# When operands from and for DRAM are loaded in a split-precision encoder block: three places in the order of DMA loads

## The chip, the cores and the metric

The kernel runs on one core of a Trainium2 chip. The time is the device time in microseconds (us) from start to end of one execution; of several executions the median is given. The engines are named as the profile names them: PE is the matrix engine (PEld its weight loads), DVE the vector engine, ACT the scalar engine, POOL the engine that runs GpSimd's work, SP the one that here only issues DMA transfers. Each engine works its own list of instructions strictly in order and waits on semaphores where an operand isn't there yet. DMA transfers are issued by SP and POOL, also in the order of their lists.

## The reference

One encoder block on x of 1024 rows by 1024 columns, float32. Cut to its core:

```python
x = layer_norm(DN_ALPHA * x + 0.5 * swiglu(x, ffn1_w_gate, ffn1_w_up, ffn1_w_down), ln1_g, ln1_b)
z = x @ w_in                                       # q, k, v, forget gates, and the RG-LRU's columns
fox = forgetting_attention(q, k, v, fg)            # 8 heads of 64, causal, logits + cum[t] - cum[s]
lru = gelu(z[..., LG_OFF:LG_OFF + LRU_W]) * rg_lru(causal_depthwise_conv(z[..., LX_OFF:LX_OFF + LRU_W]))
mix = concatenate([fox, lru]) @ w_out
x = layer_norm(DN_ALPHA * x + mix, ln2_g, ln2_b)
x = layer_norm(DN_ALPHA * x + 0.5 * swiglu(x, ffn2_w_gate, ffn2_w_up, ffn2_w_down), ln3_g, ln3_b)
# swiglu: (silu(x @ w_gate) * (x @ w_up)) @ w_down, with a hidden width of 4096
```

## The kernel before

**Arithmetic.** Every float32 operand is split into a high part (a cast to fp32r on ACT, about 0.62 us for 128x512) and a low part (the operand less its high part, on DVE, about 0.69 us). A product of two operands is three matmuls, high by high, high by low and low by high (L163, L164, L165 of `mm3`). The big products of the two FFNs are done on quarters of the matrices with seven products instead of eight (the steps `one` to `seven`, `s1` to `s4` and `t1` to `t4` are the sums that this scheme needs). All of this loads PE, and the splits load ACT and DVE.

**FFN 1, gate and up** (`gate_up`) runs over 16 pairs of weight blocks. For a pair, `weights` loads gate's and up's raw columns (L364, 1 MB each, into one of two `raw` buffers) and makes the operands of the products from them. Pair 0 has a function of its own, `first_pair`, whose order on PE, DVE and ACT is the order of the code (`manual_schedule`): the helper `put` makes a high part at L385 and notes the low part, which `do` makes later at L391. L443 copies a transposed block of x to SBUF, L449 adds two such blocks. Everywhere else a list scheduler of the framework orders the instructions of each engine, by the program's order and by what it expects of the instructions' times. `issue_after(x)` tells it to put what is made inside behind x.

**Work for later, spread over the pairs.** `prepare` is a generator (`steps`). Between its yields it makes, in small pieces, the operands of FFN 2's pair 0 and writes them to DRAM (`pre_d`), then the split halves of one part of W_out and writes these to DRAM as well (`wo_d`). A step loads a small tile (`aux`, L272), subtracts (L290, L296, L302, L307), splits it in `halves` and stores it through POOL's DMA queue (L285, L317). `gate_up` takes a step after `two` and after `five` of gate and of up, in each pair from pair 1 on.

**Attention** (`attention`) is a loop over 64 units (h, i): head h, block i of 128 query rows. The scores of a unit are made three units ahead of its values (`AHEAD`). `probs` makes the scores on PE (L1158, L1159), masks a part of `cum` on POOL (L1162), adds and takes the minimum on DVE (L1164), and takes the exponential on ACT (L1165). `to_pT` transposes the probabilities (PE L1179) and splits them (ACT L1183, DVE L1184). `values` multiplies them with v (PE L1200), and adds up in `o` (ACT L1203, DVE L1204). When a pair of heads is done, its output is scaled (L1188, L1209, L1210) and split into a `mix` (ACT L1212, and L1213 on POOL or DVE), which is stored to `mix_d` by POOL's queue (L1216). The heads' inputs q, k, v and `cum` are loaded on SP ahead of the head (L1139 to L1144).

Within the loop there is other work to fill PE: up to unit 35, tiles of the product of the RG-LRU's half with W_out; near the end, `out_tile`, the product of the stored mixes with W_out's other half. For it `ready_out_w` (L1119) loads the split parts of W_out from `wo_d`, two tiles of 512 KB for each of four parts, in the eight `ws` buffers that the fill tiles had before. Units 40, 50 and 52 (`MIXES`) load the three stored mixes (L1269), and unit 52 also loads the scale and shift of norm 2 (`load_gb`, L102 for the scale, L105 for the shift, tiles named `gb`); POOL then multiplies the scale by -1 (L192). The last loads of `gb` are remembered as `self.fetched`.

**FFN 2, gate and up** begins after the attention with `ready_pair`, which fetches the operands of pair 0 from `pre_d` (L556): "11", "21" and "t1" into `ws` tiles, "t4" and "t2" into the two `raw` buffers.

Of the kernel before, what the change touches and what calls it, by code (L numbers as in the profile page):

```python
# [10 lines left out]
F32R = mybir.dt.float32r  # L11
# [6 lines left out]
P = 128  # L18
# [41 lines left out]
class Block:  # L60
# [273 lines left out]
    def gate_up(self, wg, wu, h_d, rows, bank, tp, wsp, raws=None, later=None, aside=None, ready=None, steps=None):  # L334
# [4 lines left out]
        nc, v = self.nc, self.nc.vector  # L339
# [4 lines left out]
        def two_blocks():  # L344
            return block(F32R), block(F32R)
# [15 lines left out]
        def weights(pair, view, w):  # L361

            r = self.raw([P, KT, 2 * P])
            nc.sync.dma_start(r, view[:, :, pair * 2 * P:(pair + 1) * 2 * P])  # L364
            b11, b12, b21, b22 = quarters(r)
            w["11"] = parts(b11)
            w["21"] = parts(b21)
            t1 = less(b12, b11)
            t2 = less(b22, t1)
            w["t2"] = parts(t2)  # L370
            w["t1"] = parts(t1)
            w["t3"] = parts(less(b22, b12))
            w["22"] = parts(b22)
            w["t4"] = parts(less(b21, t2))
# [171 lines left out]
        def ready_pair(g, u):  # L546

            both = g, u
            r1, r2 = rows[0:4], rows[4:NT]

            def place(name, j):
                return tuple(x[:, :, j * P:(j + 1) * P] for x in A[name])

            def fetch(n, m, to):
                for l in range(2):
                    nc.sync.dma_start(f32(to[l]).rearrange("p (h k) f -> p h k f", h=2),  # L556
                                      ready[both.index(m), OPERANDS.index(n)].rearrange("h p (l k) f -> l p h k f", l=2)[l])
                m.w[n] = to

            for n in ("11", "21", "t1"):  # L560
                for m in both:
                    fetch(n, m, two_blocks())
            for n in ("t4", "t2"):
                r = self.rawp.tile([P, 4, 4, P], F32R, tag="raw", name=self.nm("raw"))
                for i, m in enumerate(both):
                    fetch(n, m, (r[:, 2 * i], r[:, 2 * i + 1]))
            t21 = [block() for _ in range(4)]
            g.sum, u.sum = self.sum_bank(), self.sum_bank()
            g.product("11", "11", g.sum, True)
            u.product("11", "11", u.sum, True)  # L570
            s = [block() for _ in range(4)]
            a22, two = {}, {}
            for n, j in enumerate((3, 2, 1, 0)):
                nc.scalar.copy(t21[j], self.transposed(r2[j], 0, bank))
                a22[j] = self.transposed(r2[j], 1, bank)
                v.tensor_tensor(s[j], a22[j], t21[j], ALU.add)
                parts(s[j], place("s1", j))
                if n < 2:
                    m = both[n]
                    nc.scalar.copy(m.s1, m.sum)  # L580
            two[g] = g.product("21", "12")
            parts(a22[3], place("22", 3))
            two[u] = u.product("21", "12")
            v.tensor_tensor(g.c[0], two[g], g.s1, ALU.add)
            for j in (2, 1, 0):
                parts(a22[j], place("22", j))
            g.z = g.product("t1", "s1")
            u.z = u.product("t1", "s1")
            v.tensor_tensor(u.c[0], two[u], u.s1, ALU.add)
            for m in both:  # L590
                fetch("t3", m, two_blocks())
            nc.scalar.copy(g.s5, g.z)
            four = {g: g.product("t4", "22")}

            def s2(j):
                v.tensor_tensor(s[j], s[j], unsplit(r1[j], 0), ALU.subtract)
                parts(s[j], place("s2", j))

            def s3(j):
                v.tensor_tensor(t21[j], unsplit(r1[j], 0), t21[j], ALU.subtract)  # L600
                parts(t21[j], place("s3", j))

            for j in range(4):
                s2(j)
            four[u] = u.product("t4", "22")
            nc.scalar.copy(u.s5, u.z)
            nc.scalar.copy(g.c[2], four[g])
            s3(0)
            s3(1)
            g.product("t2", "s2", g.sum)  # L610
            nc.scalar.copy(u.c[2], four[u])
            u.product("t2", "s2", u.sum)
            s3(2)
            s3(3)
            for m in both:
                nc.scalar.copy(m.u, m.sum)
            for j in range(4):
                v.tensor_tensor(s[j], unsplit(r1[j], 1), s[j], ALU.subtract)
                parts(s[j], place("s4", j))
            for m in both:  # L620
                fetch("22", m, two_blocks())
            g.product("t3", "s3", g.sum)
            u.product("t3", "s3", u.sum)

            def add_seven(m):
                v.tensor_tensor(m.c[3], m.sum, m.s5, ALU.add)
                v.tensor_tensor(m.c[2], m.c[2], m.sum, ALU.add)

            for m in both:
                m.product("22", "s4", m.z)  # L630
                add_seven(m)
            for m in both:
                v.tensor_tensor(m.c[1], m.z, m.u, ALU.add)
# [48 lines left out]
        for pair in range(FF // P // 2):  # L682
            if pair == 0:
                g0, h0, first, fifth, g1, h1, u = (self.row() for _ in range(7))
                homes = list(zip(halves(first), halves(first), halves(fifth)))
                gate, up = Matrix((g0, g1), *homes[0]), Matrix((h0, h1), *homes[1])
            else:
                g0, g1, uu, h0, h1, u = (self.row() for _ in range(6))
                gate, up = (Matrix(r, r[1][:, 0:H], x, r[0][:, H:]) for r, x in zip(((g0, g1), (h0, h1)), halves(uu)))
            def finish(pair=pair, g=(g0, g1), h=(h0, h1), u=u):  # L690
                for x, y in zip(h, g):
                    v.tensor_tensor(x, x, y, ALU.mult)
                (a11, a21), (a12, a22) = (halves(x) for x in h)
                s5 = g[0][:, 0:H]
                v.tensor_tensor(u[:, 0:H], a11, a22, ALU.add)
                v.tensor_tensor(u[:, H:], a21, a22, ALU.add)  # L696
                v.tensor_tensor(s5, a11, a12, ALU.add)
                v.tensor_tensor(a21, a21, a11, ALU.subtract)
                v.tensor_tensor(a12, a12, a22, ALU.subtract)
                d = h_d[pair // 4][:, pair % 4].rearrange("r p t -> p r t")  # L700
                for n, t in enumerate((*h, u)):
                    nc.gpsimd.dma_start(d[:, 2 * n:2 * n + 2], t.rearrange("p (r t) -> p r t", r=2))  # L702
                return nc.gpsimd.dma_start(d[:, 6], s5)

            def end(pair=pair, finish=finish):
                store = finish()
                if aside is not None and pair == 2:
                    with self.tc.issue_after(store.ins):
                        aside()

            if pair == 0:
                if ready is not None:
                    ready_pair(gate, up)
                else:
                    with self.tc.manual_schedule(engines=ENGINES):
                        first_pair(gate, up)
                silu((g0, g1))
                end()
                continue
            for m, view in zip((gate, up), self.gu_views(wg, wu)):  # L720
                weights(pair, view, m.w)
            for m in (gate, up):
                m.one()
                if pending:
                    pending()
                for step in ("two", "six", "five", "seven", "three"):
                    getattr(m, step)()
                    if steps and step in ("two", "five"):
                        next(steps, None)

                def pending(m=m, gate=gate, g=(g0, g1), end=end, last=pair == FF // P // 2 - 1):
                    m.four()
                    if m is gate:
                        silu(g)
                    elif not last:
                        end()
# [385 lines left out]
    def attention(self, w_out, mixp, ln, normed):  # L1122

        nc, v = self.nc, self.nc.vector
# [5 lines left out]
        with self.pool("att_p", 3) as pp, self.pool("att_t", 1) as tp, self.pool("att_pt", 6) as ptp, self.pool("att_qk", 2, side="right") as qkp:  # L1130
# [110 lines left out]
            for n in range(len(units) + AHEAD + 1):  # L1241
                if n < len(units):
                    h, i = units[n]
# [10 lines left out]
                for m in due(n - 1):  # L1254
                    h, i = units[m]
# [4 lines left out]
                if fill and (n < 2 or n % 8 in (2, 3, 4)):  # L1260
                    i, d = fill.pop(0)
                    with self.tc.issue_after(scores.ins) if n < 3 else nullcontext():
                        self.down_tile(i, lru_tiles, 1.0, (d,))
                if 45 <= n < 53 and n % 2:
                    w_fox.append(next(w_steps))
                if n in MIXES:
                    mix.append(tuple(self.hp.tile([P, T], F32R, tag="h", name=self.nm("mix")) for _ in range(2)))
# [147 lines left out]
```

## Time and profile before

| | |
|---|---|
| median of 3 runs | 2323.25 us (2322.42 to 2323.91) |
| the profiled execution | 2323.19 us |
| its span, first to last instruction | 2321.5 us |
| mean granted clock of PE | 0.997 |
| DVE busy | 1635.6 us (70%) |
| ACT busy | 1019.1 us (44%) |
| POOL busy | 227.8 us (10%) |
| DMA, mean over the span | 139 GB/s |

The page of the profile lists busy times, the chain of work that ended last, and groups of instructions. Views of the trace show the instructions of an engine in a window (the timeline: start, duration, engine, line, operation, output<-input, shapes, how often in a row, and in brackets how long the engine had been idle and what ended it), the waits of an engine in sums (total, how many, the longest), busy time by stretch with the granted clock of PE (the share of full speed), and the chain of waits. L12 is line 12 of the kernel before. Rows with DMA_DIRECT2D on SP or POOL are issues of transfers; the chain shows how long such a transfer took to land. The first pair runs from about 10 to 60 us of the span, the attention from about 1170 to 1345 us.

### The profile page before, as it was taken

What the parts mean: (1) busy time and instruction counts of PE and PEld (TensorE: products, weight loads), DVE (VectorE), ACT (ScalarE), POOL (GpSimd) and SP (SyncE); (2) the same over time, 40 slices, a digit from 0 to 9 for tenths busy, and PEclk for the clock granted to TensorE, in tenths of its full rate; (3) what the DMA queues carried; (4) which work ended last, traced back from release to release, by engine and by line L of the source; (5) the groups of instructions that cost most, each with busy time, mean ns of one, the idle gap of its engine ahead of it and who ended that gap; (6) DMA issues with size and microseconds to landing.
All of it is one profiled execution on the core that took longest, in us unless ns stands there. A gap on an engine that the chain in (4) does not pass through costs nothing.

```text
span 2321.5 us, 28560 instructions
## 1 busy us (share of the span) xinstructions
PE 2298.7 (99%) x10705; PEld 1914.1 (82%) x10705; DVE 1635.6 (70%) x2521; ACT 1019.1 (44%) x1623; POOL 227.8 (10%) x388
## 2 busy tenths in 40 slices
PE   8999999999999999999999999999999999999998
PEld 7888888888888888888898788888888888888887
DVE  7867666666467788866667899565656665577886
ACT  5443434343344345453556755334333333344341
POOL 0121111100000000111133210000000000000000
PEclk9999999999999999999999999999999999999999
DMA  4444444433276433233274934232323232564542
GB/s 150 141 141 145 139 147 141 146 113 125 101 259 234 147 127 109 75 92 110 91 218 126 283 137 141 86 118 89 122 93 123 87 118 87 195 244 168 182 144 73
DMA packets 194444, 323.08 MB, mean 139 GB/s; under 512 B 10033, under 2 KB 115825, under 8 KB 194305
## 3 DMA queue, kind: packets, MB, share of 16 engines
q1 hardware_dynamic: 167712, 230.74, 30.9%
q0 software_dynamic: 26592, 90.51, 9.9%
q8 instruction: 84, 1.38, 0.3%
q14 instruction: 56, 0.45, 0.1%
HBM read 226.81 MB, written 94.40 MB: 138 GB/s over the span
## 4 chain that ended last, share of the span: by engine, by line
PE 81%; issue 10%; DVE 3%; DMA 3%; POOL 2%; ACT 1%; SPq 0%; POOLq 0%; DVEq 0%; ACTq 0%
PE x L163 7%; PE x L164 7%; PE x L165 7%; PE s L165 6%; PE s L164 6%; PE s L163 6%; PE a L165 6%; PE a L164 6%; PE a L163 6%; PE b L163 6%; PE b L164 6%; PE b L165 6%; PE a L1200 1%; PE a L1179 1%; PE a L1049 1%
## 5 line engine op out<-in xcount | busy, mean ns | idle before, releaser
L349 ACT CAST ws<-t 128x512 fp32r<-128x512 f32 x240 | 148.9, 623 | 374.2 <-PE b L164 253.0
L349 ACT CAST ws<-raw 128x512 fp32r<-128x512 f32 x180 | 111.0, 622 | 239.3 <-PE x L164 237.3
L350 DVE TENSOR_TENSOR ws<-t,ws 128x512 fp32r<-128x512 f32 x240 | 164.3, 686 | 56.4 <-ACT ws L349 50.6
L350 DVE TENSOR_TENSOR ws<-raw,ws 128x512 fp32r<-128x512 f32 x180 | 123.3, 688 | 114.4 <-ACT ws L349 110.3
L164 PE MATMUL a<-ws,ws 128*128 128x512 f32 x512 | 199.8, 390 | 0.2
L163 PE MATMUL a<-ws,ws 128*128 128x512 f32 x512 | 199.3, 390 | 0.4 <-ACT row L672 0.4
L163 PE MATMUL b<-As,ws 128*128 128x512 f32 x512 | 199.4, 389 | 0.2 <-ACT row L663 0.2
L164 PE MATMUL b<-As,ws 128*128 128x512 f32 x512 | 199.3, 389 | 0.0
L165 PE MATMUL b<-As,ws 128*128 128x512 f32 x512 | 199.2, 389 | 0.0
L165 PE MATMUL a<-ws,ws 128*128 128x512 f32 x512 | 199.2, 389 | 0.0
L163 PE MATMUL x<-As,ws 128*128 128x512 f32 x504 | 196.6, 390 | 2.1 <-ACT row L659 2.0
L164 PE MATMUL x<-As,ws 128*128 128x512 f32 x504 | 196.1, 389 | 0.0
L165 PE MATMUL x<-As,ws 128*128 128x512 f32 x504 | 196.1, 389 | 0.0
L163 PE MATMUL x<-A,ws 128*128 128x512 f32 x496 | 193.3, 390 | 0.0
L165 PE MATMUL x<-A,ws 128*128 128x512 f32 x496 | 193.0, 389 | 0.0
L164 PE MATMUL x<-A,ws 128*128 128x512 f32 x496 | 193.0, 389 | 0.0
L772 ACT CAST ws<-raw 128x1024 fp32r<-128x1024 f32 x112 | 117.4, 1050 | 157.8 <-PE a L164 87.2
L775 DVE TENSOR_TENSOR ws<-raw,ws 128x1024 fp32r<-128x1024 f32 x112 | 136.6, 1220 | 53.0 <-ACT ws L772 52.6
L702 POOL DMA_DIRECT2D h_d<-row x96 | 68.9, 719 | 968.5 <-DVE row L696 928.4
L163 PE MATMUL s<-ws,ws 128*128 128x512 f32 x384 | 149.5, 389 | 0.0
L165 PE MATMUL s<-ws,ws 128*128 128x512 f32 x384 | 149.4, 389 | 0.0
L164 PE MATMUL s<-ws,ws 128*128 128x512 f32 x384 | 149.4, 389 | 0.0
(295 smaller groups left out, 5252.7 us busy)
## 6 DMA issues: line engine op xcount, KB each, us to landing
raw<-h_d SPq DMA_DIRECT2D x56, 1024.0 KB, 5.4
h_d<-row POOLq DMA_DIRECT2D x96, 512.0 KB, 3.5
wd<-in_ffn_w_down_dram SPq DMA_DIRECT2D x32, 1024.0 KB, 7.5
raw<-in_ffn_w_gate_dram SPq DMA_DIRECT2D x30, 1024.0 KB, 5.3
raw<-in_ffn_w_up_dram SPq DMA_DIRECT2D x30, 1024.0 KB, 5.3
h_d<-row POOLq DMA_DIRECT2D x32, 256.0 KB, 2.7
raw<-in_w_in_dram SPq DMA_DIRECT2D x16, 512.0 KB, 4.9
pre_d<-ws POOLq DMA_DIRECT2D x28, 256.0 KB, 2.7
```

What stands on the lines that cost most here:

```text
L163: mm(out, ah, bh, start=first, stop=False, skip_group_check=goes_on)
L164: mm(out, ah, bl, start=False, stop=False, skip_group_check=goes_on)
L165: mm(out, al, bh, start=False, stop=last, skip_group_check=goes_on)
L349: nc.scalar.copy(hi, src)
L350: v.tensor_tensor(lo, src, f32(hi), ALU.subtract)
L702: nc.gpsimd.dma_start(d[:, 2 * n:2 * n + 2], t.rearrange("p (r t) -> p r t", r=2))
L772: cast = nc.scalar.copy(hi, src)
L775: self.mark = v.tensor_tensor(lo, src, f32(hi), ALU.subtract)
L1049: nc.tensor.matmul(pa[:, 0:width], xh, wh[:, 0:width], start=k == 0, stop=False)
L1179: nc.tensor.transpose(pa[:, (j % 4) * P:(j % 4 + 1) * P], p[:, j * P:(j + 1) * P], self.ident)
L1200: mm(pv[:, ps], vt[:, j, :], pts[h, qt][j // 4][l][:, j % 4, ps], start=j == 0 and l == 0, stop=j == last and l == 1)
```

## The change

```diff
@@ def gate_up: weights
-            nc.sync.dma_start(r, view[:, :, pair * 2 * P:(pair + 1) * 2 * P])
+            self.weight_load = nc.sync.dma_start(r, view[:, :, pair * 2 * P:(pair + 1) * 2 * P])
@@ def gate_up: ready_pair
-            for n in ("11", "21", "t1"):
-                for m in both:
-                    fetch(n, m, two_blocks())
-            for n in ("t4", "t2"):
-                r = self.rawp.tile([P, 4, 4, P], F32R, tag="raw", name=self.nm("raw"))
-                for i, m in enumerate(both):
-                    fetch(n, m, (r[:, 2 * i], r[:, 2 * i + 1]))
+            with self.tc.issue_after(self.fetched.ins):
+                for n in ("11", "21", "t1"):
+                    for m in both:
+                        fetch(n, m, two_blocks())
+                for n in ("t4", "t2"):
+                    r = self.rawp.tile([P, 4, 4, P], F32R, tag="raw", name=self.nm("raw"))
+                    for i, m in enumerate(both):
+                        fetch(n, m, (r[:, 2 * i], r[:, 2 * i + 1]))
@@ def gate_up: the loop over pairs
                     if steps and step in ("two", "five"):
-                        next(steps, None)
+                        with self.tc.issue_after(self.weight_load.ins):
+                            next(steps, None)
@@ def attention
-                if 45 <= n < 53 and n % 2:
+                if 36 <= n < 40:
                     w_fox.append(next(w_steps))
```

There are three edits. A step of `prepare` that is taken in a pair is put behind the last raw load of that pair. The fetches of `ready_pair` are put behind the last load of `gb`. And the four parts of W_out are asked for at units 36 to 39 instead of units 45, 47, 49 and 51. No instruction is added to the computation or taken from it. The scheduler, which has new bounds and a new program order, moves further instructions.

**The first pair, on SP.** Transfers at the start of the kernel, in the order in which SP issues them: x's rows, the first two `aux` tiles of `prepare`, and pair 1's raw columns (`raw_669` of gate, `raw_707` of up). Before:

```order
L1316 DMA x_27_134<-in_x_dram 128x1024
L272 DMA aux_773<-in_ffn_w_gate_dram 128x2x128
L272 DMA aux_775<-in_ffn_w_gate_dram 128x2x128
L364 DMA raw_669<-in_ffn_w_gate_dram 128x8x256
L364 DMA raw_707<-in_ffn_w_up_dram 128x8x256
L364 DMA raw_954<-in_ffn_w_gate_dram 128x8x256
```

And on SP with the change, at the same place:

```order
L1318 DMA x_27_134<-in_x_dram 128x1024
L364 DMA raw_669<-in_ffn_w_gate_dram 128x8x256
L364 DMA raw_707<-in_ffn_w_up_dram 128x8x256
L272 DMA aux_773<-in_ffn_w_gate_dram 128x2x128
L272 DMA aux_775<-in_ffn_w_gate_dram 128x2x128
L364 DMA raw_954<-in_ffn_w_gate_dram 128x8x256
```

The two `aux` loads stand behind the two raw loads of pair 1, which need the `raw` buffers that pair 0 reads. (Lines in the changed kernel are up to two higher.)

**The first pair, on DVE.** The subtractions of `prepare` (L290) and of the first pair, before:

```order
L391 TENSOR_TENSOR ws_176<-raw_135,ws_175 128x512
L391 TENSOR_TENSOR ws_178<-raw_136,ws_177 128x512
L290 TENSOR_TENSOR aux_775<-aux_775,aux_773 128x256
L391 TENSOR_TENSOR ws_180<-t_261,ws_179 128x512
L355 TENSOR_TENSOR t_289<-raw_135,t_261 128x512
```

With the change L290 stands on DVE among the sums of pair 1's operands (L355), 64 positions later:

```order
L350 TENSOR_TENSOR ws_676<-raw_669,ws_675 128x512
L355 TENSOR_TENSOR t_679<-raw_669 128x512
L290 TENSOR_TENSOR aux_775<-aux_775,aux_773 128x256
L355 TENSOR_TENSOR t_681<-raw_669,t_679 128x512
L544 TENSOR_TENSOR row_167<-b_632,row_164 128x512
```

Nothing of `prepare` is left in the first pair on DVE; the order of the first pair's own instructions is as it was.

**The end of the attention, on SP.** Loads of W_out's parts (`w`), of a stored mix (`mix`) and of head 6 (`q`, `kh`, `kl`, `cum`, `v`). Before, from the first mix on:

```order
L1269 DMA mix_11083<-mix_d 128x1024
L1269 DMA mix_11084<-mix_d 128x1024
L1119 DMA w_11254<-wo_d 128x1024
L1119 DMA w_11255<-wo_d 128x1024
L1140 DMA kh_11106<-k_d 64x1024
L1139 DMA q_11105<-q_d 64x1024
```

With the change SP's order at that place is:

```order
L1121 DMA w_10980<-wo_d 128x1024
L1121 DMA w_10981<-wo_d 128x1024
L1121 DMA w_11005<-wo_d 128x1024
L1121 DMA w_11006<-wo_d 128x1024
L1121 DMA w_11043<-wo_d 128x1024
L1121 DMA w_11044<-wo_d 128x1024
L1121 DMA w_11063<-wo_d 128x1024
L1121 DMA w_11064<-wo_d 128x1024
L1271 DMA mix_11099<-mix_d 128x1024
L1271 DMA mix_11100<-mix_d 128x1024
L1141 DMA q_11121<-q_d 64x1024
L1142 DMA kh_11122<-k_d 64x1024
```

All eight loads of W_out's parts stand ahead of the first mix and of head 6; before, the other six came after head 6's and head 7's loads.

**The end of the attention, on POOL.** Masks of head 6 and head 7 (`cum_11104` and `cum_11358` before, `cum_11120` and `cum_11366` with the change), copies of the scaling of an output (`gate_raw`), and the scaling of `gb` (L192). Before:

```order
L1162 AFFINE_SELECT cum_11104<-cum_11104 128x128
L1162 AFFINE_SELECT cum_11358<-cum_11358 128x128 x2
L1188 COPY gate_raw<-wfr 128x256
L192 TENSOR_SCALAR gb_11523<-gb_11523 128x1024
L1162 AFFINE_SELECT cum_11104<-cum_11104 128x128
```

With the change, on POOL:

```order
L1164 AFFINE_SELECT cum_11120<-cum_11120 128x128
L192 TENSOR_SCALAR gb_11523<-gb_11523 128x1024
L1164 AFFINE_SELECT cum_11366<-cum_11366 128x128 x2
L1190 COPY gate_raw<-wfr 128x256
L1164 AFFINE_SELECT cum_11120<-cum_11120 128x128
```

The scaling of `gb` stands ahead of two masks of head 7, those of its blocks 4 and 3, and ahead of the copy, where it stood behind all three.

**The other loads from pre_d.** The eight loads of "t4" and "t2" stood on SP among the loads of the first three heads, at two places of four; with the change they stand behind the loads of `gb`. On PE, DVE and ACT, head 6's first scores and what follows from them come 16 PE rows later, behind head 5's last values and transposes.

## The prediction

> **What bounds the kernel now.** I read the first part of the page, then the waits of TensorE, and then, at each place that the change touches, the timelines of the engines there.
>
> ```profile
> PE 2298.7 (99%) x10705; PEld 1914.1 (82%) x10705; DVE 1635.6 (70%) x2521; ACT 1019.1 (44%) x1623; POOL 227.8 (10%) x388
> ```
>
> TensorE (PE) is busy for 2298.7 of the span's 2321.5 us, so at most some 23 us could be saved without taking matmuls away, and the change takes none away. Every microsecond in which PE is held up anywhere is added to the end, and every idle stretch that goes is taken from it. The sum is thus a sum over idle stretches of PE. The waits of PE say which are worth looking at:
>
> ```profile
> PE b L163 <- ACT ws L443: 2.8, 1, 2.8
> PE s L1158 <- DVE m L1164: 2.4, 7, 0.9
> ```
>
> The largest is a single stretch of 2.8 us behind a copy of L443 in the first pair; the second is spread over seven places in the attention. The change reaches both.
>
> **First pair: the aux loads behind pair 1's raw loads.** On DVE, the subtraction L290 leaves the first pair (position 16 of its order) for pair 1 (position 80). Views: the timelines of DVE, ACT and PE, with the start, the duration and the work, and in brackets the idle time before it.
>
> ```profile
> 15.62 1.29 DVE L391 TENSOR_TENSOR ws<-raw,ws 128x512 fp32r<-128x512 f32 x2
> 19.57 0.43 DVE L290 TENSOR_TENSOR aux<-aux,aux 128x256 f32<-128x256 f32 x1 [2.66 <-DMA aux<-in_ffn_w_gate_dram]
> 19.91 0.68 DVE L391 TENSOR_TENSOR ws<-t,ws 128x512 fp32r<-128x512 f32 x1
> ...
> 22.32 1.28 DVE L449 TENSOR_TENSOR ws<-b,ws 128x512 f32<-128x512 f32 x2
> ```
>
> ```profile
> 19.33 0.60 ACT L443 COPY ws<-b 128x512 f32<-128x512 f32 x1
> 23.04 0.62 ACT L385 CAST As<-ws 128x512 fp32r<-128x512 f32 x1 [3.11 <-DVE ws L449]
> 23.56 0.58 ACT L443 COPY ws<-b 128x512 f32<-128x512 f32 x1
> ```
>
> ```profile
> 17.73 3.66 PE L249 MATMUL b<-ident,x 128*128 128x128 f32 x32
> 24.19 0.50 PE L163 MATMUL b<-A,ws 128*128 128x512 f32 x1 [2.80 <-ACT ws L443]
> ...
> 25.71 0.63 PE L163 MATMUL b<-A,ws 128*128 128x512 f32 x1
> ```
>
> DVE stands still for 2.66 us until an aux tile has landed. Behind it everything is late in a row: L449 at 22.32, ACT's cast at 23.04, ACT's next L443 at 23.56, and PE, whose transposes ended at 17.73 + 3.66 = 21.39, gets its bank only at 24.19. Without L290 the DVE row of 19.91 follows the pair of 15.62, less the usual 0.08 of overlap, at 16.83: DVE gains 3.08. L449 then starts at 19.24, the cast at about 19.96 (ACT is free at 19.93), L443 at 20.48, and the bank is free at about 21.1, ahead of 21.39. So PE's stretch of 2.80 goes.
>
> PE gains something besides. Right behind the stretch stand rows of 0.63 us where the others have 0.39:
>
> ```profile
> 22.20:25.60 3.40, 1.41 (x6) 1.20 (x7) 3.31 (x7) 2.56 (x5) 0.00 (x0) 1.00 0.00 0
> 25.60:29.00 3.40, 3.40 (x10) 2.67 (x9) 2.96 (x5) 2.63 (x6) 0.00 (x0) 0.50 0.00 0
> 29.00:32.40 3.40, 3.40 (x16) 2.79 (x16) 2.84 (x6) 0.00 (x0) 0.00 (x0) 1.00 0.00 0
> ```
>
> In these stretches the busy times of PE, PEld, DVE, ACT and POOL are followed by the granted clock: 1.00, then 0.50, then 1.00. At half clock PE did 10 matmuls where it does 16 otherwise, which is 6 x 0.23, or about 1.5 us. I read this as the answer to the pause, so it goes too. PE alone would gain 2.80 + 1.5 = 4.3 us.
>
> But PE isn't alone here. At the end of the first pair DVE delivers just in time (DVE's row, PE's row, and from the view of L436 on DVE what it had waited for between 28 and 32, in us and times):
>
> ```profile
> 56.97 0.68 DVE L391 TENSOR_TENSOR As<-ws,As 128x512 fp32r<-128x512 f32 x1
> ```
>
> ```profile
> 57.71 0.50 PE L164 MATMUL b<-As,ws 128*128 128x512 f32 x1
> ```
>
> ```profile
>   PE b L165: 0.9, 2
> ```
>
> DVE's last operand is done at 57.65 and PE's row that reads it starts at 57.71, with no slack. DVE comes forward by 3.08 and by what its own two waits for PE (0.9 us) shrink, since PE is earlier by more than DVE. I take about half of these: **-3.5 us**. Bounds: -2.9 (nothing of the waits, and some of L290's 0.43 us comes back as lateness in pair 1, where DVE is packed) and -4.3 (PE's whole gain).
>
> In pair 1, L290 stands between two L355. Its loads leave SP behind the two raw loads, of which this is the second:
>
> ```profile
> 50.30 0.39 SPq L364 DMA_DIRECT2D raw<-in_ffn_w_up_dram  x1
> ```
>
> ```profile
> 62.47 0.69 DVE L355 TENSOR_TENSOR t<-raw,t 128x512 f32<-128x512 f32 x1
> ```
>
> ```profile
> 11.03 8.45 DMA aux<-in_ffn_w_gate_dram
> ```
>
> Issued at about 51 in before's time, with the 8.45 us that they took in the chain of waits, they land near 59.5, ahead of 62. No wait comes back; only 2 to 3 us of slack stand against it. The other pairs keep their order.
>
> **Gate/up 2's operands behind norm 2's vectors.** Eight raw loads from pre_d move on SP from two places in the early attention to behind the loads of gb.
>
> ```profile
> 1162.95 2.03 SPq L556 DMA_DIRECT2D raw<-pre_d  x4
> 1172.13 0.47 SPq L1139 DMA_DIRECT2D q<-q_d  x1
> ```
>
> Behind the first four SP has 7.1 us of free time up to 1172.13, where it waits for something else; behind the other four it stands likewise before head 2's loads. Leaving them out gains nothing. At their new place they follow the last loads of the attention, and nothing but gate/up 2, far behind the attention, reads them. **0 us**, with -0.3 to +0.3 for the lighter and the fuller DMA engines.
>
> **W_out's parts at units 36 to 39.** The eight w loads (512 KB each) now all stand ahead of mix 0 and of head 6; two stood there before. Six more are 3.1 MB. What is late behind them, and what on POOL:
>
> ```profile
> 1298.93 9.90 DMA cum<-cum_d
> ...
> 1324.10 9.28 DMA mix_d<-mix
> 1333.40 4.76 DMA mix<-mix_d
> ```
>
> ```profile
> 1335.20 0.29 POOL L1162 TENSOR_SCALAR_AFFINE_SELECT cum<-cum 128x128 f32<-128x128 f32 x1 [1.65 <-DVE m L1164]
> ...
> 1340.59 1.05 POOL L192 TENSOR_SCALAR gb<-gb 128x1024 f32<-128x1024 f32 x1 [2.23 <-DMA gb<-in_ln_g_dram]
> ```
>
> ```profile
> 1307.00:1311.50 4.50, 4.18 (x30) 3.56 (x29) 3.71 (x15) 3.62 (x12) 1.89 (x5) 1.00 1.06 388
> ```
>
> First, head 6 comes later. At 388 GB/s, with a DMA share of 1.06, 3.1 MB take 8 us; about one of them falls into time in which SP waited anyway. Head 6's cum lands near 1316 instead of 1298.93 + 9.90 = 1308.8. Part of that is covered by head 5's last values and transposes, which PE's new order puts ahead (16 rows, some 4.6 us). I estimate PE 2.5 us late at about 1327.
>
> Second, and this decides: in the new order POOL does the scaling of gb (L192) ahead of the masks of units (7, 4) and (7, 3), where before it came behind them. POOL works in order, so these masks now wait for gb's landing. Behind the mask stand on DVE and PE:
>
> ```profile
> 1335.65 0.81 DVE L1164 CUSTOM_DVE_ANT_0 p<-s,cum 128x640 f32<-128x640 f32 x1
> ...
> 1338.10 0.54 DVE L1213 TENSOR_TENSOR mix<-o,mix 128x256 fp32r<-128x256 f32 x1 [0.30 <-ACT mix L1212]
> ```
>
> ```profile
> 1338.54 0.39 PE L163 MATMUL a<-w,mix 128*128 128x512 f32 x1
> ```
>
> The loads ahead of gb carry the same bytes in both kernels through full DMA engines, so gb lands at about the same time. Then L192 starts at 1340.6, the mask 1.0 later, and p of unit (7, 4) at 1342.0 instead of 1335.65. PE's row of 1338.54 comes 2.89 after p; less DVE's idle 0.30, which the delay swallows, it starts at about 1344.5: 5.9 us later. The 2.5 us of the first step lie inside this. I take 0.6 us off, since mix 2's store (9.28 us) had four w loads beside it and now has none: **+5.3 us**. Bounds: 2.5 if gb lands in time, 8.4 if the store is no faster (below).
>
> Third, PE pauses for 2.8 to 5.3 us there. By the rows of 25.6 to 29.0 a pause of 2.80 us was followed by a stretch of half clock that cost 1.5 us: **+1.5 us** (0 to 2).
>
> Beside these rows stands a rule. The Trainium skill, "TensorE: Matmul & The Clock Gate", in "What's actually happening", says that the clock is halved after at least one idle window of about 3.4 us. By that rule the pause of 2.80 us would not have been the cause of the 0.50, and a pause in the attention shorter than that would cost nothing further; the row speaks for the shorter pause, being one case only.
>
> **The sum.** -3.5 + 0 + 5.3 + 1.5 = +3.3 us. The profiled execution took 2323.19 us (its span is 2321.5), and the median of the runs is 2323.25, so both give **2326.5 us**, 0.14% slower. About 0.2%, or 4.65 us, is what a measurement of this kernel can tell from no change; the bounds are 2318.6 and 2327.9.
>
> **Rivals.**
> - *The gb chain is carried along (slower).* Mix 2's store starts when PE and ACT have made mix 2, and PE is 2.5 us late there. Were the store and the load no faster than 9.28 and 4.76, gb would land at about 1343.1 and the second step be +8.4 in place of +5.3: 2329.6. It decides from a landing of gb after 1342. For it: the fixed order store, load, gb on SP. Against it: the w loads beside the store are gone.
> - *No half clock.* If a pause below some threshold doesn't lower the clock, or the pause falls into two pieces, the 1.5 us go: 2325.0. Against it stands the row of 0.50.
> - *gb in time (faster).* If the DMA engines, freed of the w loads, bring gb before the masks are due (about 1335), only -3.5 is left, or less by what head 6 costs: 2319.7 to 2322.2. Against it: the same 4 MB lie ahead of gb, and gb landed 5 us after 1335.
> - *The first pair doesn't gain.* If the aux loads, behind 2 MB of raw loads, land after 62, the stall of 2.66 comes back in pair 1: 2329.
>
> **How the numbers follow.** Forecast 0.45; gb chain carried along 0.2; no half clock 0.2; gb in time 0.1; no gain in the first pair 0.05. The range leaves out the lower part of "gb in time" and the top of the carried chain: 2320.0 to 2329.8. Slower than 2327.9: the carried chain, the failed first pair, and some of the forecast's own upper bounds, 0.3. Faster than 2318.6: a full gain of 4.3 us and gb in time together, with some of what I have overlooked, 0.08. The rest, 0.62, is within 0.2%.
>
> **What would show it.** In the new profile, PE's wait for L443 of 2.8 us must be gone, DVE must have no L290 before 25, and the clock in 25.6 to 29.0 must be 1.00; PE's row of 57.71 must stand near 54.2. L192 on POOL must stand ahead of a mask with a wait for gb before it, DVE's p of 128x640 must start near 1342 less 3.5, and PE must have a wait for DVE or ACT of 2.8 us or more near there, with a clock below 1.00 behind it. The prediction is wrong if PE has other work during the wait for the mask, if gb lands much sooner, or if DVE has slack that I overlooked at the end of the first pair.

## The result, and the profile after

| | before | with the change |
|---|---|---|
| median of 17 runs | 2323.13 us (2320.59 to 2325.56) | 2327.31 us (2324.43 to 2330.32) |
| the profiled execution | 2323.19 us | 2326.57 us |

The ratio is 1.0019, with a 95% interval of 1.0012 to 1.0026: the change makes the kernel 4.2 us slower, a little under 0.2%. The forecast was 2326.5 us, 0.14% slower, so it is 0.8 us too low. The prediction took 0.2% for the least that can be told from no change; with 17 runs on each side the interval leaves out 1, so the loss is clear of the noise though it lies inside that band.

The first line of the page, and two lines of PE's waits (total in us, how many, the longest), with the change:

```profile
span 2324.9 us, 28562 instructions
```

```profile
PE s L1160 <- DVE m L1166: 2.7, 6, 1.3
PE a L163 <- ACT mix L1214: 2.5, 1, 2.5
```

The wait of 2.8 us for L443 is gone. In its place stands a single wait of 2.5 us for a mix at the end of the attention, and the waits for L1166 (L1164 before) add up to 2.7 us, against 2.4. A count of PE's matmuls in the two traces shows where the time comes and goes. PE has the same 10705 matmuls in both kernels, so the start of its n-th matmul can be set beside the start of the n-th one of before (the order differs in a few dozen places of the attention):

| PE's matmul number | start before, us | change less before, us |
|---|---|---|
| 60, in the first pair | 15.9 | +0.49 |
| 150, first pair, behind the pause | 36.3 | -4.18 |
| 2000, down product of FFN 1 | 457.3 | -4.57 |
| 6150, attention, ahead of head 6's first scores | 1306.4 | -4.38 |
| 6300, attention, ahead of the mix products | 1331.2 | +0.74 |
| 6400, behind the scaling of gb | 1348.2 | +3.28 |
| 10704, the last | 2313.0 | +3.41 |

So there is a gain of 4.2 to 4.7 us in the first 40 us, and a loss of 7.7 us in the attention, in two pieces: 5.1 us at head 6, and 2.5 us at gb. Nothing else in this table moves by more than 0.4 us.

**The first pair.** The timeline of DVE, then that of PE, then the stretches that were shown of before (busy times of PE, PEld, DVE, ACT, POOL, then the clock):

```profile
17.09 0.69 DVE L391 TENSOR_TENSOR ws<-t,ws 128x512 fp32r<-128x512 f32 x1
...
19.50 0.69 DVE L449 TENSOR_TENSOR ws<-b,ws 128x512 f32<-128x512 f32 x1
...
52.79 0.69 DVE L391 TENSOR_TENSOR As<-ws,As 128x512 fp32r<-128x512 f32 x1
```

```profile
53.53 0.51 PE L164 MATMUL b<-As,ws 128*128 128x512 f32 x1
```

```profile
22.20:25.60 3.40, 3.40 (x17) 2.80 (x16) 3.31 (x7) 2.82 (x7) 0.00 (x0) 1.00 0.00 0
25.60:29.00 3.40, 3.40 (x17) 2.81 (x16) 3.40 (x6) 0.54 (x2) 0.00 (x0) 1.00 0.00 0
```

L391 follows the pair before it at once, L449 starts 2.82 us sooner, and PE has no pause at all in these stretches; the clock stays at 1.00 where it was 0.50. DVE's last operand of the pair comes at 52.79 instead of 56.97, 4.18 us sooner, and PE's row follows it.

**Head 6.** SP issues all eight w loads ahead of it; the rows of SP behind them show what that does to the queue:

```profile
1282.56 4.22 SPq L1121 DMA_DIRECT2D w<-wo_d  x8
1288.02 1.56 SPq L1271 DMA_DIRECT2D mix<-mix_d  x2
1292.87 0.45 SPq L1141 DMA_DIRECT2D q<-q_d  x1
1295.29 0.45 SPq L1142 DMA_DIRECT2D kh<-k_d  x1
1296.63 0.45 SPq L1143 DMA_DIRECT2D kl<-k_d  x1
1297.88 0.45 SPq L1141 DMA_DIRECT2D q<-q_d  x1
1299.09 0.44 SPq L1142 DMA_DIRECT2D kh<-k_d  x1
```

An issue takes 0.45 us, but the next one follows after 1.2 to 1.3 us, and behind the first of q only after 2.4 us (0.64 us before, with 0.59 us for an issue). SP itself is held up: the trace puts its waits ahead of the issues of q, kh and kl (8.4 us in all between 1280 and 1320) down to landings of the w loads. The second half of kh, issued at 1299.09, takes 11.05 us to land (before, issued at 1297.60, it took 9.0). Three of the issues of before, and the mask on POOL that waits for cum with the change:

```profile
1296.97 0.59 SPq L1139 DMA_DIRECT2D q<-q_d  x1
1297.60 0.59 SPq L1140 DMA_DIRECT2D kh<-k_d  x1
1298.24 0.59 SPq L1141 DMA_DIRECT2D kl<-k_d  x1
```

```profile
1312.92 0.29 POOL L1164 TENSOR_SCALAR_AFFINE_SELECT cum<-cum 128x128 f32<-128x128 f32 x1 [2.48 <-DMA cum<-cum_d]
```

PE then has these waits:

```profile
1310.38 0.70 PE L1160 MATMUL s<-kh,q 128*128 128x512 f32 x2 [1.15 <-DMA kh<-k_d]
...
1314.56 0.51 PE L1160 MATMUL s<-kh,q 128*128 128x512 f32 x1 [1.30 <-DVE m L1166]
...
1321.35 1.52 PE L1181 MATMUL a<-ident,p 128*128 128x128 f32 x9 [1.05 <-DVE pt L1186]
```

The second of these goes back to cum by way of that mask. Behind the first two waits comes a stretch of half clock:

```profile
1317.00:1318.50 1.50, 1.50 (x8) 1.47 (x8) 1.06 (x3) 1.50 (x5) 0.29 (x1) 0.50 1.03 208
1318.50:1320.00 1.50, 1.50 (x7) 1.34 (x6) 0.23 (x1) 0.97 (x4) 0.00 (x0) 0.50 1.00 265
```

**The scaling of gb.** POOL, DVE and PE:

```profile
1337.92 1.04 POOL L192 TENSOR_SCALAR gb<-gb 128x1024 f32<-128x1024 f32 x1 [3.53 <-DMA gb<-in_ln_g_dram]
1338.94 0.28 POOL L1164 TENSOR_SCALAR_AFFINE_SELECT cum<-cum 128x128 f32<-128x128 f32 x1
```

```profile
1339.25 0.82 DVE L1166 CUSTOM_DVE_ANT_0 p<-s,cum 128x640 f32<-128x640 f32 x1 [2.68 <-POOL cum L1164]
```

```profile
1341.56 0.50 PE L163 MATMUL a<-w,mix 128*128 128x512 f32 x1 [2.45 <-ACT mix L1214]
```

This is the chain that the prediction describes, row by row: gb lands, L192 takes 1.04 us, the mask of unit (7, 4) 0.28 us, DVE's p follows, and PE's product of a mix is 2.45 us late. No stretch of half clock follows this pause: the clock is 1.00 from 1340 to 1350.

### The profile page after: what moved, and what is told of

The parts are those of the page before. It is cut to its first block, busy times and chain, and to the rows that moved or that the text cites. A ratio compares the mean times of both kernels' runs of the same rounds, so it can differ in the third digit from the quotient of the medians.

```text
span 2324.9 us, 28562 instructions
## 1 busy us (share of the span) xinstructions
PE 2300.4 (99%) x10705; PEld 1915.3 (82%) x10705; DVE 1636.4 (70%) x2521; ACT 1019.8 (44%) x1623; POOL 227.8 (10%) x388
## 4 chain that ended last, share of the span: by engine, by line
PE 83%; issue 9%; DVE 3%; DMA 2%; POOL 2%; ACT 1%; SPq 0%; POOLq 0%; DVEq 0%; ACTq 0%
PE x L163 8%; PE x L164 8%; PE x L165 8%; PE s L165 6%; PE s L164 6%; PE s L163 6%; PE b L163 6%; PE b L164 6%; PE b L165 6%; PE a L163 6%; PE a L165 6%; PE a L164 6%; PE a L1202 1%; PE a L1181 1%; PE a L1051 1%
```

## The experiments

The theory from the two traces: the first-pair edit gains its 4.2 us and more and keeps them; the fetches of `ready_pair` do nothing; the W_out edit loses 5 us by head 6's late loads and 2.5 us by POOL's order. The main rivals: that some of this belongs to another edit, that the order on POOL only shows a lateness that would be there anyway, or that the bytes don't matter. Medians are given as differences from the median of before in the same batch (2323.66 us for the first four runs, 2322.88 us for the others). The 11 or more runs of one kernel spread by 4 to 7 us, and an interval of a ratio is about 0.0009 to each side, 2 us (0.0014, or 3 us, for the W_out edit alone, which has 5 runs).

**The first-pair edit alone.** The `issue_after(self.weight_load.ins)` around `next(steps, None)`, and nothing else of the change.

> Only the edit on prepare's steps (behind their pair's raw loads); the fetches of ready_pair and the units of W_out's parts are as before. The traces of before and of the change show the end of the first pair 4.2 us earlier (PE's row of 57.71 at 53.53). Theory A, the gain is kept to the end because PE is the bound: 2323.1 - 4.2 = 2318.9 us (2318.0 to 2319.8). Rival B, DVE is packed in the pairs that follow and gives part of it back: 2320.5 to 2322.5. In the profile A expects the last pairs' rows and the attention 4 us earlier than before, and the waits of PE at the end of the attention as they were before.

Measured: 2318.31 us, -5.3 us (ratio 0.9979, 0.9970 to 0.9988). Theory A; the median is a little below its 2318.9. In the profile matmul 150 is 4.24 us early, but the attention starts 3 us early and not 4: 1.5 us are lost in FFN 1, where PE's waits for L659 add up to 1.8 to 3.7 us in the traces of the kernels. From there to the end nothing changes (-2.96 at matmul 6150, -3.08 at the last). The gain is kept.

**The W_out edit alone.**

```diff
-                if 45 <= n < 53 and n % 2:
+                if 36 <= n < 40:
```

> Only the W_out edit (units 36 to 39). Theory A: the attention loses what the change's trace shows between 1282 and 1342, 5.0 us ahead of the scaling of gb and 2.2 us at it, 7.4 us in all with the drift behind it: 2323.1 + 7.4 = 2330.5 us (2329.5 to 2331.5). Rival B: a part of the loss belongs to the eight loads from pre_d that the change puts behind gb; then this run is under 2328.5. Rival C: the delays of the first pair's end shift the attention against the DMA queues, so that W_out's move alone costs less than 5.

Measured: 2334.28 us, +10.6 us (ratio 1.0046, 1.0033 to 1.0060, from 5 runs). That is more than theory A's 7.4 and above its range, and against both rivals: the whole loss is there without the edit on the fetches. The waits are in the same places and longer:

```profile
1315.68 0.70 PE L1158 MATMUL s<-kh,q 128*128 128x512 f32 x2 [2.23 <-DMA kh<-k_d]
...
1320.59 0.50 PE L1158 MATMUL s<-kh,q 128*128 128x512 f32 x1 [2.04 <-DVE m L1164]
```

and a clock below 1.00 follows both pauses, that at head 6 and that at gb (a wait of 2.57 us there):

```profile
1320.20:1323.60 3.40, 2.86 (x13) 2.49 (x13) 2.40 (x6) 2.72 (x5) 0.72 (x3) 0.65 1.03 211
```

```profile
1348.00:1351.40 3.40, 3.40 (x11) 2.56 (x10) 2.06 (x4) 0.48 (x1) 0.00 (x0) 0.58 0.00 0
```

With the first-pair edit beside it the W_out edit costs about 4.2 + 5.3 = 9.5 us by the medians, so the two edits add up within the intervals. Two things make this trace lose more than that of the change: head 6's cum lands 1.8 us later here, counted from the issue of v ahead of the w loads (the second half of kh 1.1 us later), and the pause at gb is followed by half clock, where in the change it isn't. Why the loads land later the runs don't show; on the clock see the last section.

**The first-pair edit and the fetches of `ready_pair`.**

> The first-pair edit and the fetches of ready_pair behind gb; W_out's parts at their old units. Theory A: the fetches cost and gain nothing, so this equals the run with the first-pair edit alone within 0.7 us, near 2318.9. Rival B: the eight pre_d loads, now in one heap at 1331, slow gb's landing or the last mixes and cost 1 us or more (2320 and up). Rival C: the attention's early loads, freed of them, gain 1 us or more (under 2318).

Measured: 2318.74 us, -4.9 us (0.9981, 0.9972 to 0.9990), 0.4 us from the first-pair edit alone, with intervals of 2 us on each. Theory A: moving the eight pre_d loads neither gains nor costs anything that can be measured.

**The whole change with the scaling of gb behind one mask.**

```diff
-                nc.gpsimd.affine_select(cum[:, ts], cum[:, ts], pattern=[[-1, P]], compare_op=ALU.is_ge, fill=1e30, base=0, channel_multiplier=1)
+                masks[h, i] = nc.gpsimd.affine_select(cum[:, ts], cum[:, ts], pattern=[[-1, P]], compare_op=ALU.is_ge, fill=1e30, base=0, channel_multiplier=1)
...
+                if n == 57:
+                    with self.tc.issue_after(masks[7, 4].ins):
+                        scale()
```

`load_gb` only loads here, and `scale` is its multiplication by -1 on POOL.

> All of the change, and the scaling of gb on POOL issued behind the mask of unit (7, 4), so that this mask no longer waits for gb's landing. Theory A, the order on POOL costs 2.2 us of its own: 2327.3 - 2.2 = 2325.1 us (2324.3 to 2325.9), and PE's wait of 2.45 us ahead of a mix product near 1341 is gone. Rival B, the third mix lands late as well and takes the wait's place (PE waits for a mix from mix_d there): 2326.5 to 2327.5. Rival C, the unit behind it (7, 3) waits in its place and PE loses the same a few rows later: no change.

Measured: 2324.55 us, +0.9 us (1.0005, 0.9996 to 1.0013), 2.8 us faster than the change by the medians, 3.3 us by the differences from before. Theory A: PE's wait ahead of the mix product is gone and nothing takes its place. L192 (L193 here) waits for gb as before, but the mask has gone by:

```profile
1334.45 0.29 POOL L1168 TENSOR_SCALAR_AFFINE_SELECT cum<-cum 128x128 f32<-128x128 f32 x1 [1.65 <-DVE m L1170]
1337.46 1.23 POOL L193 TENSOR_SCALAR gb<-gb 128x1024 f32<-128x1024 f32 x1 [2.71 <-DMA gb<-in_ln_g_dram]
```

By the count of matmuls the attention loses 3.3 us here (7.7 in the change), all of it at head 6, where the change loses 5.1. The waits at 1310 and 1314 are nearly the same (0.90 and 1.29 us), but no half clock follows them in this execution. So the edit is worth 2.6 us at gb, and that head 6 costs 1.8 us less goes with the clock. (This execution loses 1.1 us again in FFN 2, far behind the edit.)

**W_out's parts at units 43 to 46** (`if 43 <= n < 47`).

> The change with W_out's parts at units 43 to 46. On SP two of the eight loads stand ahead of head 6, as before the change, and the other six between head 6 and head 7; on POOL the scaling of gb keeps the change's place ahead of the masks of units (7, 4) and (7, 3). So the two parts of the loss in the attention are separated: head 6's lateness goes, the order on POOL stays. Theory A, both are real and independent: head 6's first scores on PE wait less than 0.6 us; the mask of (7, 4) waits for gb, which without the w loads beside mix 2's store lands 1 to 3 us sooner than in the run with the first-pair edit alone; PE loses 1 to 4 us there: 2319.6 to 2322.6. Rival B, the order on POOL costs only where head 6 was late: 2318.6, as without the W_out edit. Rival C, six loads ahead of head 7 make head 7 late and cost as much as they did ahead of head 6: 2323 and up.

Measured: 2321.9 us, -1.0 us (0.9992, 0.9983 to 1.0001). The time lies in theory A's range, but not for its reason. Head 6 waits 0.70 us; rival C is right that the six loads now ahead of head 7 cost there, though not in full: PE waits for DVE, for kh and for DVE again, some 3 us in all.

```profile
1320.02 0.87 PE L1181 MATMUL a<-ident,p 128*128 128x128 f32 x6 [1.15 <-DVE pt L1186]
1324.63 0.71 PE L1160 MATMUL s<-kh,q 128*128 128x512 f32 x2 [1.00 <-DMA kh<-k_d]
```

Theory A fell on gb: L192 stands ahead of the mask of (7, 4) and starts at 1338.08, as late as in the change, and PE waits for nothing there. The reason is in DVE's order, which the scheduler made anew:

```profile
1338.95 0.45 DVE L1215 TENSOR_TENSOR mix<-o,mix 128x256 fp32r<-128x256 f32 x1 [0.48 <-ACT mix L1214]
1339.99 0.69 DVE L229 SCALAR_TENSOR_TENSOR row<-a,row 128x512 f32<-128x512 f32 x1 [0.59 <-PE a L165]
1340.60 0.81 DVE L1166 CUSTOM_DVE_ANT_0 p<-s,cum 128x640 f32<-128x640 f32 x1
```

Here p of unit (7, 4) stands behind the mix, not ahead of it, so nothing that PE needs soon waits behind the mask.

**Four loads ahead of head 6 instead of eight** (`if n in (36, 37, 49, 51)`), two more than before.

> The change with W_out's parts at units 36, 37, 49 and 51: four of the eight loads ahead of mix 0 and head 6 instead of eight (two before), and POOL's order at gb as before. A dose for head 6's lateness: two more loads instead of six. Theory A, the price goes with the bytes ahead of head 6: a third of the 5 us and less than a window of half clock, 2318.6 + 1.7 = 2320.3 us (2319.5 to 2321.5). Rival B, there is slack ahead of head 6 that takes the first 1 MB: 2318.0 to 2319.2. Rival C, the full price comes with the place ahead of mix 0, not with the bytes: 2323.

Measured: 2320.77 us, -2.1 us (0.9990, 0.9981 to 0.9998). That is 2.8 to 3.2 us behind the two kernels without the W_out edit; the count of matmuls in the profile gives 0.9 us in the attention (-4.07 at matmul 6150, -3.18 at 6400), with PE's waits of 0.25 and 0.62 us for kh and kl. Rival C falls; between A (1.7 us) and B (at most 0.6 us) the medians are for A, but with intervals of 2 us on each, and 0.9 us in the trace, they don't settle it.

**The parts at units 43 to 46, and the scaling behind the mask.**

> As the run with the parts at units 43 to 46, and the scaling of gb behind the mask of unit (7, 4). Theory A: both losses of the attention are gone, 2318.6 us (2317.6 to 2319.8), and it is faster than that run by what PE waited behind that mask. Rival B, six loads ahead of head 7 cost by themselves: 2320 and up.

Measured: 2321.83 us, -1.1 us (0.9993, 0.9985 to 1.0002): the same as with the scaling ahead of the mask, as DVE's order there lets one expect. Rival B: what is left is head 7's lateness (waits of 1.15, 1.01, 0.84 and 0.87 us).

**The parts at units 47, 49, 51 and 53, and the scaling behind the mask.**

> The change with W_out's parts at units 47, 49, 51 and 53 (on SP one part ahead of head 6, one between the heads, one behind mix 1 and one behind gb) and the scaling of gb behind the mask of unit (7, 4). Theory A, what is loaded ahead of head 7, the mixes and gb is what makes PE wait at the end of the attention (0.58 + 0.93 + 0.54 us of waits are left there without the W_out edit): 0.5 to 1.5 us less than without the W_out edit, 2317.1 to 2318.1. Rival B, those waits come from the work on DVE and ACT and not from loads: 2318.6. Rival C, the last part, now behind gb, is late for the first mix products: 2320 and up.

Measured: 2323.14 us, +0.3 us (1.0000, 0.9991 to 1.0009). Rival C: the last part lands too late.

```profile
1337.82 0.47 PE L163 MATMUL a<-w,mix 128*128 128x512 f32 x1 [2.82 <-DMA w<-wo_d]
```

The waits of 0.58, 0.93 and 0.54 us are there as well, with one part fewer ahead of head 7's mixes, so they don't come from these loads. None of the kernels is faster than the first-pair edit alone, which beats both kernels of the case: about 5 us faster than before, 9 us faster than the change.

## Why the prediction was right

- *The first pair* was put at -3.5 us (-2.9 to -4.3); the traces of the kernels that have the edit show -3.9 to -4.8 at matmul 150. The mechanism is as said. The size was set too small at one term: of DVE's waits for PE I took half, and nearly all went. In the change's trace between 19 and 53 DVE waits for 0.25, 0.17 and 0.16 us, each time for ACT; its three waits for PE in this stretch of before (0.35 and 0.56 us, and 0.42 us at 38.34, which the sum didn't have) are gone. L290 in pair 1 (at 58.17) waits for nothing, as worked out: its loads were in time.
- *Half clock in the first pair* goes with the pause. All kernels with the edit have 1.00 from 22 to 32; before and the W_out edit alone, which keep the pause (2.80 and 3.08 us), have a stretch below 1.00 right behind it.
- *The fetches of `ready_pair`*: 0 us predicted, 0.4 us measured, inside the noise of 2 us.
- *Head 6* is the step that was mis-sized. I had PE 2.5 us late and took that to lie inside the wait for gb. It is 5.1 us late with half clock, 3.3 us without it (the run with the scaling behind the mask), and gb comes on top. The landing of cum was about right (POOL's first mask of head 6 starts at 1312.92 in the change; with the first pair's 4.4 us added that is 1317.3, against my 1316). But I followed cum alone: kh and kl of the second half are held up by SP's slower issue as well, and PE waits for kh first (1.15 us), for the first p of head 6 next, and then runs at half clock.
- *The scaling of gb* was put at +5.3 us with head 6's share inside. The chain is shown by its rows and by its removal (-2.8 us by the medians, -2.6 us by the count of matmuls). In the change it costs 2.6 us of its own, since PE comes to it 5.1 us late, not 2.5. The total of both steps, 7.7 us with half clock, was put at 6.8.
- *Half clock in the attention* was forecast behind the wait for gb, at 1.5 us, and came behind head 6's waits instead; with it head 6 costs 1.8 us more than without. Of the signs that the prediction named, two are missing: PE's wait at gb is 2.45 us, not 2.8 or more, and no clock below 1.00 is behind it.
- That the sum came out so close (+3.3 said, +3.4 in the profile, +4.2 by the medians) is in part luck: the gain was put 0.7 us too small and the loss about 0.9 us too small, and the two misses cancel. That there are two terms, of which sign, and through which instructions, was right.
- *The rival that gb's chain is carried along* falls in part, and here too, two misses work against each other: head 6's lateness and the store were both put too small. In absolute time mix 2's store was issued 0.5 us later than before and gb landed 2.7 us sooner; with the first pair's 4.4 us added that is 4.9 us and 1.7 us later. I took 0.6 us off for the store, which no longer has w loads beside it. Its second half took 5.05 us where it took 9.28, so it won 4.2 us, and gb's own load gave back 1.0 (7.8 us instead of 6.7). So of the 4.9 us at the store 1.7 reached gb.

## What to carry to other kernels

When one engine is 99% busy, list its idle stretches and work the change out as a sum over them; here two terms of opposite sign, each of 4 to 8 us in 2300, were found that way from the order of DMA issues. Loads that are asked for earlier than they are needed go through the same queue as those that are needed now: look first at what stands behind them on the issuing engine, and at the rate of issue as well as at the bytes. What an instruction that waits costs is decided by what stands behind it on its own engine, and then by the order on the next engine: the same wait of POOL cost PE 2.5 us where DVE had the consumer of the mask ahead of the mix, and nothing where DVE had it behind.

## What the runs showed of the hardware that was not expected

Pauses of PE of nearly the same length were answered differently by the clock: 2.80 and 3.08 us in the first pair and 2.57 us at gb (W_out edit alone) were followed by a stretch at half clock, 2.45 us (the change) and 2.82 us (the last run) were not. Several short waits close together (1.15 and 1.30 us) were followed by one as well, in the change but not in the run with the scaling behind the mask, where they were 0.90 and 1.29 us.

The traces show what the difference goes with. The stretches at half clock in them last 3.41 us, those at the very end of a trace apart, and within one execution their starts lie whole multiples of 3.413 us apart: in before 25.61 lies 5 of them behind 8.54, where the first such stretch begins, and with the W_out edit alone 1321.22 and 1348.53 lie 380 and 388 behind 24.16. So each execution can be cut into windows on its own grid. PE's busy time in such a window, and the clock in the one behind it:

| kernel | window, us | PE busy, of 3.41 us | clock in the next |
|---|---|---|---|
| W_out edit alone, first pair | 20.75 to 24.16 | 0.55 | 0.50 |
| W_out edit alone, gb | 1345.12 to 1348.53 | 0.90 | 0.50 |
| W_out edit alone, head 6 | 1317.81 to 1321.22 | 1.37 | 0.50 |
| before, first pair | 22.20 to 25.61 | 1.42 | 0.50 |
| the change, head 6 | 1313.16 to 1316.57 | 1.81 | 0.50 |
| parts at 43 to 46, scaling behind the mask | 1314.98 to 1318.39 | 1.87 | 1.00 |
| the last run, first half of the 2.82 us | 1333.02 to 1336.43 | 1.98 | 1.00 |
| the last run, second half | 1336.43 to 1339.84 | 2.02 | 1.00 |
| the change, gb, first half of the 2.45 us | 1337.05 to 1340.46 | 2.06 | 1.00 |
| the change, gb, second half | 1340.46 to 1343.87 | 2.31 | 1.00 |
| scaling behind the mask, head 6 | 1313.59 to 1317.00 | 2.36 | 1.00 |

The pauses of 2.45 and 2.82 us fell across the border of two windows, and neither window was idle enough; that of 2.57 us fell almost whole into one. It is the same with the short waits: that of 1.30 us in the change lies inside one window, that of 1.29 us in the other run across a border. It also tells why the half clock of before begins 1.4 us after the pause has ended. The order isn't kept at the two ends of the kernel: 1.91 us at 5.17 to 8.58 (four loads ahead of head 6) was followed by half clock, 1.61 us at 2312.47 to 2315.88 (parts at 43 to 46) was not. No run moved a pause on purpose, so there is no sharp bound here. The Trainium skill, "TensorE: Matmul & The Clock Gate", in "What's actually happening", describes a free-running window of about 3.4 us. The traces agree with such a window and its length, but one that was idle for 1.6 us of 3.41 (the change, head 6) was enough.

Where the grid lies differs from one execution to the next (half clock from 25.61 in one, from 24.16 in another, behind nearly the same pause), so whether a pause of 1.3 to 2.8 us pays the price of half clock, about 1.5 us, can't be said ahead of the run. A forecast should carry it as a chance.
